# Expert weights with permuted rows, loaded in longer runs of HBM

## The chip, the cores and the metric

The kernel runs on one core of a Trainium2 chip, in one launch. The metric is the time of an execution on the device in microseconds (us). The core has five engines that run beside each other: TensorE (PE; its weight loads are listed apart as PEld), VectorE (DVE), ScalarE (ACT), GpSimd (POOL) and SyncE (SP), which here issues nearly all transfers. Sixteen DMA engines move the data between HBM and the core's on-chip memory (SBUF); matrix products land in PSUM. All data are float32.

## The reference, cut to what matters

Two blocks are applied to 256 tokens of 1024 channels, and each ends with a mixture of experts. The first has 16 experts with 256 inner channels, the second 32 experts with 512; each token goes to two experts of one group. Cut to the experts:

```python
for e in range(N_EXPERTS):
    act = jax.nn.silu(t @ w_gate[e]) * (t @ w_up[e]) * gates[:, e:e + 1]
    y = y + act @ w_down[e]
```

Here `t` holds the normalised tokens (in block 2 also scaled and shifted by columns that a modulation vector gives), `w_gate[e]` and `w_up[e]` are 1024 x 256 (block 2: 1024 x 512) and `w_down[e]` is 256 x 1024 (512 x 1024). Gate and up sum over the 1024 channels, down over the inner channels; a sum doesn't depend on the order of its terms.

## The kernel before, in words

The program works in stages: token mixing of block 1 (0 to about 150 us of the profile), its experts (to about 316 us), token mixing of block 2 (to about 840 us), and its experts (to the end). All experts' weights are streamed from HBM once, whatever the routing says.

**The lists.** For each expert the tokens' places in a list of 64 are worked out (`moe`, line 917, up to line 1009), which leaves PE partly idle at the start of both stages. `dispatch` (line 1062) gathers the listed tokens of four experts by a product with one-hot matrices: `xh` and `xl` are the normalised rows split in two parts (lines 926, 1000 and 1003, by ACT, POOL and DVE), and the result `xt[:, k, :]` holds 128 channels on the partitions for each of eight values of k. On the way out it is scaled by the norm column `gcol[:, k]` and, in block 2, shifted by `bcol[:, k]`.

**The products.** Experts are taken in pairs. `gate_up` (line 1111) forms gate and up from eight products over k for each of the two experts, then `act` (line 1131, DVE). `turn` (line 1134) transposes `act`, `down` (line 1142) multiplies by the down weights for two halves n of 512 output channels, each a sum over NF = 2 or 4 values of f, and `combine` (line 1162) adds the parts to the four sums `y` in PSUM. The order on PE is: gate and up of a pair, then the down product of the pair before it (`lower`, line 1194).

**The stream.** `Stream` (line 497) keeps the list of weight pieces of 1 MiB in the order of their use and issues their loads from SP, eight pieces ahead of the one that is wanted (`take`, line 541). A piece lies in a slot of 8 KB per partition of pool `gp`, which has 19 slots (NG) for all large tiles; a load waits until its slot is free. `load1` and `load2` (lines 550 and 557) say which rows of a weight matrix go to which partition: row 128 k + p to partition p, place k. So a partition reads single rows that lie 128 rows apart: 1 KB each for block 1's gate and up, 2 KB for block 2's gate and up, and 4 KB for block 1's down. Block 2's down weights are cut in two pieces by output columns, which makes 2 KB again; the first column half of `down` needs only the first piece of each expert. Slots are given out in the order of the loads, and SP issues in order. The last two pieces are loaded by halves in turn (line 527).

**The modulation.** `ada_job` (line 594) forms 512 of the modulation's values by products, turns them into columns by four transposes on PE (line 609) and adds the four parts and a bias on DVE (lines 610 and 611). Twelve of these jobs exist; numbers 6 to 8 run at the start of block 1's experts, where PE waits for the routing, number 9 in block 2's token mixing.

Of the kernel before, what the change touches and what calls it, by code (L numbers as in the profile page):

```python
# [122 lines left out]
def _body(es, tc, I, cst_d, msk_d, out_d, tap, stop):  # L123
# [73 lines left out]
    nA += 2  # L197
    colG = cp.tile([128, 8], F32, name="colG")
# [16 lines left out]
    def wload(ap, shape, name="w"):  # L215
        t = U(name, shape)
        SY.dma_start(t, ap)
        return t

    def piece(w, r0, nk, c0, n):  # L220
        """A piece of weights, split exactly into two parts that the PE array multiplies in one pass each."""
        hi = U("hi", [nk, n], F32R)
        lo = U("lo", [nk, n], F32R)
        for a in range(2):
            ks = slice(nk // 2 * a, nk // 2 * (a + 1))
            t = sp.tile([128, nk // 2, n], F32, tag="st4", name="w", bufs=NST)
            SY.dma_start(t, w[r0 + 64 * nk * a:r0 + 64 * nk * (a + 1), c0:c0 + n].rearrange("(k p) n -> p k n", p=128))
            t2["hi"] = A.activation(hi[:, ks], t, AF.Copy)  # L228
            t2["lo"] = V.tensor_tensor(lo[:, ks], t, hi[:, ks].bitcast(F32), op=ALU.subtract)  # L229
        return hi, lo  # L230

    class Jobs:
        """Products in the order of their use; the weights of the next ones are loaded and split ahead."""
# [22 lines left out]
        def ch(self, w, c0, h, n, evac):  # L256
            """out[channel, token]: evac(c, psum) for two groups of 128 channels."""
# [17 lines left out]
        def row32(self, w, c0, h, evac):  # L275
            """The same for two tiles, in float32 as it stands."""
# [15 lines left out]
        def row(self, w, c0, h, tiles, evac, n=512, keep=None, reuse=None, more=None):  # L292
            """out[token, channel]: evac(j, psum) for the tiles of 128 tokens."""
# [49 lines left out]
    def weave(main, sides, rate):  # L343
        """Traces main, with rate steps of the side chains between two of its steps."""
        due = 0.0
        sides = list(sides)
        for _ in main:
            due += rate
            while due >= 1.0 and sides:
                due -= 1.0  # L350
                g = sides.pop(0)
                try:
                    next(g)
                    sides.append(g)
                except StopIteration:
                    pass
        return sides
# [21 lines left out]
    def rms_h(x, behind=None):  # L379
        """The same, by halves of the rows."""  # L380
# [15 lines left out]
    def rms_r(x):  # L396
        """1 / root mean square of each row."""
# [30 lines left out]
    def transpose_split(x, r, hi, lo, off, gcol, bcol=None, ps=None, dg=None):  # L428
        """Rows scaled by r, transposed by a product with the diagonal of r."""
# [12 lines left out]
    class Router:  # L442
        """Logits of the experts, from the halves of the rows as they come."""
# [53 lines left out]
    class Stream:  # L497
        """Weight pieces of expert pairs, loaded in the order of their use and ahead of it."""
# [24 lines left out]
        def ahead(self, n):  # L523
            while self.n < min(n, len(self.order)):
                p, k, s, i = self.order[self.n]
                ap, shape = self.ap[p][k][s][i]
                if self.ends and self.n == len(self.order) - 2:
                    # the last two by halves in turn
                    two = [(U("w", shape), self.ap[p][k][q][i][0]) for q in range(2)]
                    for h in range(2):  # L530
                        for q, (t, ap) in enumerate(two):
                            SY.dma_start(t[:, 2 * h:2 * h + 2], ap[:, 2 * h:2 * h + 2])
                            self.t[(p, k, q, i)] = t
# [16 lines left out]
    def load1(e, kind):  # L550
        w = wsel(I[{"g": "w_gate", "u": "w_up", "d": "w_down"}[kind]], e)
        if kind == "d":
            return [(w.rearrange("(k p) n -> p k n", p=128), [2, D])]
        return [(w.rearrange("(k p) n -> p k n", p=128), [KD, 256])]

    st1 = Stream(load1, [(2 * p, 2 * p + 1) for p in range(8)])
    def load2(e, kind):
        w = wsel(I[{"g": "w_gate_2", "u": "w_up_2", "d": "w_down_2"}[kind]], e)
        wv = w.rearrange("(k p) n -> p k n", p=128)
        if kind == "d":  # L560
            return [(wv[:, :, 512 * i:512 * i + 512], [4, 512]) for i in range(2)]
        return [(wv[:, 4 * i:4 * i + 4, :], [4, 512]) for i in range(2)]

    st2 = Stream(load2, [(2 * p, 2 * p + 1) for p in range(16)], True)
    # ================= modulation and parameter columns of block 2 =================
# [13 lines left out]
    ada = cp.tile([128, 48, 2], F32, name="ada")  # L579

# [10 lines left out]
    def ada_job(jobs, b, step=False):  # L591
# [4 lines left out]
        def run(t0, t1):  # L596
# [11 lines left out]
            for c in range(4):  # L608
# [3 lines left out]
                            colC[:, oBA + 4 * b:oBA + 4 * b + 4].unsqueeze(2).to_broadcast([128, 4, 2]), op=ALU.add)  # L612
            yield
# [3 lines left out]
    # ================= block 1: token mixing =================  # L617
# [39 lines left out]
    # context tokens, normalised  # L657
# [77 lines left out]
    def conv_chain():  # L735
        # causal convolution
# [3 lines left out]
        # the last taps in another sum, by the idle engines  # L740
# [45 lines left out]
    def pool_chain():  # L786
        # windowed means
# [128 lines left out]
    # ================= mixture of experts =================  # L916
    def moe(x, E, router, gcol, bcol, st, FE, n_static, mid=None, before_if=None, gate=None, idle=None):
# [7 lines left out]
        xl = R2("xnl", F32R)  # L925
        for i in (1, 0):
            A.activation(xh[i], x[i], AF.Copy, scale=r[:, i:i + 1])
# [12 lines left out]
        # the group: first of the largest logits, and its probability  # L940
# [47 lines left out]
        # the place of each token in its expert's list  # L988
# [8 lines left out]
        for n in range(2):  # L997
# [3 lines left out]
            G.tensor_tensor(xl[1][:, cs], t, xh[1][:, cs].bitcast(F32), op=ALU.subtract)  # L1001
        with after(last_m):
            V.scalar_tensor_tensor(xl[0], x[0], r[:, 0:1], xh[0].bitcast(F32), op0=ALU.mult, op1=ALU.subtract)
# [10 lines left out]
        def spill():  # L1014
            # lists longer than CAP: further chunks
# [25 lines left out]
            # s2_ = 1 - offset of the chunk  # L1041
# [69 lines left out]
        def gate_up(gu, xt, off, wcol, half=None):  # L1111
# [19 lines left out]
            V.scalar_tensor_tensor(act, sg, wcol, outs[1], op0=ALU.mult, op1=ALU.mult)  # L1131
# [10 lines left out]
        def down(dn, aT):  # L1142
            parts = []
            for n in range(2):
                q = mm_ps("pdn")
                for f in range(NF):
                    for s in range(2):
                        pc = dn[s]
                        mm(q[64 * s:64 * s + 64, :], aT[:, f, 64 * s:64 * s + 64],
                           pc[n][:, f, :] if NF == 4 else pc[0][:, f, 512 * n:512 * n + 512], f == 0, f == NF - 1)  # L1150
# [104 lines left out]
    # ================= block 2: token mixing, its products in order =================  # L1255
# [12 lines left out]
    def mv_jobs():  # L1268
        # values of the mLSTM; first the context's, then the others
# [68 lines left out]
    def yb_job(kk):  # L1338
        # gate of the mLSTM's heads, and its output by channels
# [97 lines left out]
    y = moe(x1, 16, rt, colA[:, oFG:oFG + 8], None, st1, 256, 2, None, lambda: J2.ahead(1), idle=first_ada)  # L1437
# [8 lines left out]
    # ================= block 2: token mixing =================  # L1446
# [15 lines left out]
    # lower bounds of the forget gates  # L1462
# [40 lines left out]
    def gate_chain():  # L1503
        gA = U("gA", [4, 512])
        gB = U("gB", [4, 512])
        # rows 0-3: forward, rows 4-7: backward with time reversed; lat by columns of the grid
# [13 lines left out]
        # log sigmoid: min(x, 0) - log(1 + exp(-|x|)), the logarithm by its series in e / (2 + e)  # L1520
# [16 lines left out]
        # sums within tiles of 128  # L1537
# [54 lines left out]
    # short convolution of queries (lat by columns) and keys (lat by rows)  # L1592
# [109 lines left out]
    def gla_core(g):  # L1702
# [26 lines left out]
        for lv in range(8):  # L1729
            x = 1 << lv  # L1730
            m = 16 // x
            if x < 32:
                # within blocks of 32; both directions in one product: their keys and their queries lie in opposite halves
# [23 lines left out]
            # decay of the keys to the end of their half, of the queries from the start of theirs  # L1757
# [143 lines left out]
    V.tensor_copy(sh2, ada[:, 24:32, 0])  # L1901

# [22 lines left out]
    # ================= block 2: experts =================  # L1925
# [8 lines left out]
    y = moe(x3, 32, rt, mod2, sh2, st2, 512, 0, gate=gf[0], idle=last_ada)  # L1934
# [42 lines left out]
```

## Time and profile before

| | us |
|---|---|
| median of three runs | 1365.89 |
| lowest and highest | 1364.04, 1366.63 |
| span of the profiled execution (first to last instruction) | 1365.3 |
| PE busy, share of the span | 1269.9, 93% |
| DVE busy, ACT busy | 639.2, 432.4 |
| moved by DMA | 359.79 MB, mean 264 GB/s |

The profiled execution has no time of its own beside its span of 1365.3 us; it lies 0.6 us below the median of the runs. A matmul's end is modelled, so that "busy" on PE can cover short waits.

### The profile page before, as it was taken

The numbers are of one execution on the slowest core, as the hardware profiler recorded it, in microseconds if no ns is written. First come the engines' busy times: TensorE is split into PE (matmuls) and PEld (weight loads), VectorE is DVE, ScalarE is ACT, GpSimd is POOL, SyncE is SP. The second block draws the span as 40 slices with busy tenths as digits, with TensorE's granted clock in tenths as the row PEclk, the third lists the DMA queues.
The fourth block names the chain that finished last, engine by engine and source line by source line (L and its number), as shares of the span: only waits on it lengthen the run. The fifth ranks groups of instructions, "written<-read, shape, count | busy, mean of one in ns | idle before, by whom it ended". The sixth has DMA issues, their size and how long they took to land. (4 is left out here: it accounts for less than half of the span.)

```text
span 1365.3 us, 19881 instructions
## 1 busy us (share of the span) xinstructions
PE 1269.9 (93%) x8082; PEld 835.2 (61%) x8082; DVE 639.2 (47%) x1405; ACT 432.4 (32%) x756; POOL 37.6 (3%) x50
## 2 busy tenths in 40 slices
PE   6988899998999999999999999999998989797984
PEld 5845476666788988988988997444342424242421
DVE  6896531226388878776657665412111111111112
ACT  5735222224144745534345442111110101010101
POOL 4200100000000000000000001000000000000000
PEclk9989899999999999999999999999999999999998
DMA  8798899994332332424436679899999999999992
GB/s 266 249 337 294 276 303 360 366 341 146 108 93 62 93 93 67 142 80 124 128 93 205 235 245 353 307 389 390 390 389 387 390 390 390 390 387 390 393 390 108
DMA packets 226708, 359.79 MB, mean 264 GB/s; under 512 B 14200, under 2 KB 100385, under 8 KB 226608
## 3 DMA queue, kind: packets, MB, share of 16 engines
q1 hardware_dynamic: 217648, 355.49, 74.3%
q10 hardware_dynamic: 7952, 2.22, 0.7%
q8 instruction: 68, 1.11, 0.3%
q0 software_dynamic: 1008, 0.70, 0.2%
q14 instruction: 32, 0.26, 0.1%
HBM read 357.34 MB, written 1.05 MB: 263 GB/s over the span
## 5 line engine op out<-in xcount | busy, mean ns | idle before, releaser
L156 PE MATMUL pg<-hT,hi 128*128 128x256 f32 (+1 forms) x1024 | 233.0, 321 | 1.5 <-DVE Qg L1321 1.5
L156 PE MATMUL pgu<-w,XT 128*64 128x256 f32 (+1 forms) x1088 | 193.2, 483 | 14.5 <-DMA w<-in_w_up_dram 14.4
L156 PE MATMUL pdn<-w,actT 128*64 128x512 f32 x656 | 167.9, 597 | 10.4 <-DMA w<-in_w_down_dram 9.9
L156 PEld LDWEIGHTS pg<-hT,hi 128*128 128x128 f32 x1024 | 167.4, 188 | 16.3 <-DVE Qg L1321 1.7
L229 DVE TENSOR_TENSOR lo<-w,hi 128x1024 fp32r<-128x1024 f32 x122 | 145.8, 1219 | 47.3 <-ACT hi L228 19.4
L156 PE MATMUL pg<-hT,lo 128*128 128x256 f32 (+1 forms) x512 | 162.6, 318 | 0.0
L228 ACT ACTIVATE hi<-w 128x1024 fp32r<-128x1024 f32 x122 | 124.9, 1052 | 89.6 <-PE pr L156 32.1
L156 PEld LDWEIGHTS pgu<-w,XT 128*64 128x64 f32 x1088 | 80.8, 137 | 110.8 <-issue 68.3
L156 PE MATMUL pgg<-w,XT 128*64 128x512 f32 x512 | 134.6, 598 | 0.0
L156 PEld LDWEIGHTS pdn<-w,actT 128*64 128x64 f32 x656 | 51.0, 137 | 100.3 <-issue 78.1
L156 PEld LDWEIGHTS pg<-hT,lo 128*128 128x128 f32 x512 | 96.4, 189 | 7.4 <-issue 0.4
L1157 ACT ACTIVATE Ph<-Pg 128x512 fp32r<-128x512 f32 x32 | 20.1, 628 | 245.3 <-DVE Pg L1153 245.3
L156 PE MATMUL pr<-hi,hT 128*128 128x256 f32 (+1 forms) x384 | 91.0, 327 | 3.6 <-PEq L1231 3.6
L156 PEld LDWEIGHTS pgg<-w,XT 128*64 128x64 f32 x512 | 38.9, 137 | 71.0 <-issue 67.4
L1130 DVE TENSOR_TENSOR sgm<-sgm,pgg 128x512 f32<-128x512 f32 x16 | 11.0, 688 | 148.5 <-ACT sgm L1129 148.5
L1153 DVE TENSOR_TENSOR Pg<-pdn,g 128x512 f32<-128x512 f32 x32 | 22.1, 692 | 116.5 <-PE pdn L156 116.5
L156 PEld LDWEIGHTS pr<-hi,hT 128*128 128x128 f32 x384 | 65.5, 192 | 10.7 <-issue 4.0
L1131 DVE SCALAR_TENSOR_TENSOR act<-sgm,ws,pgu 128x512 f32<-128x512 f32 (+1 forms) x25 | 16.3, 652 | 106.7 <-PE pgu L156 106.3
L156 PE MATMUL pr<-lo,hT 128*128 128x256 f32 (+1 forms) x192 | 62.8, 327 | 0.0
L156 PE MATMUL py<-Ph,Gt 128*128 128x512 f32 x100 | 41.0, 441 | 18.4 <-ACT Ph L1157 16.9
L1139 ACT ACTIVATE actT<-pactT 128x512 f32<-128x512 f32 (+1 forms) x25 | 13.0, 519 | 132.4 <-PE pactT L1137 132.4
L156 PE MATMUL pgx<-Dd,xnh 128*128 128x256 f32 (+1 forms) x208 | 53.4, 297 | 0.3 <-DVE e L980 0.2
(515 smaller groups left out, 1934.3 us busy)
## 6 DMA issues: line engine op xcount, KB each, us to landing
w<-in_w_gate_dram SPq DMA_DIRECT2D x82, 1024.0 KB, 14.2
w<-in_w_up_dram SPq DMA_DIRECT2D x82, 1024.0 KB, 14.2
w<-in_w_down_dram SPq DMA_DIRECT2D x80, 1024.0 KB, 14.1
w<-in_w_in_dram SPq DMA_DIRECT2D x98, 512.0 KB, 4.5
w<-in_w_ada_dram SPq DMA_DIRECT2D x24, 1024.0 KB, 7.0
w<-in_w_out_dram SPq DMA_DIRECT2D x4, 1024.0 KB, 5.2
w<-in_w_branch_b_dram SPq DMA_DIRECT2D x8, 512.0 KB, 4.1
w<-in_w_branch_a_dram SPq DMA_DIRECT2D x8, 512.0 KB, 4.4
```

Source lines behind the costliest of these rows:

```text
L156: t2["mm"] = PE.matmul(out, lhsT, rhs, start=start, stop=stop, skip_group_check=True)
L228: t2["hi"] = A.activation(hi[:, ks], t, AF.Copy)
L229: t2["lo"] = V.tensor_tensor(lo[:, ks], t, hi[:, ks].bitcast(F32), op=ALU.subtract)
L1130: V.tensor_tensor(sg, sg, outs[0], op=ALU.mult)
L1131: V.scalar_tensor_tensor(act, sg, wcol, outs[1], op0=ALU.mult, op1=ALU.mult)
L1139: A.activation(aT, p, AF.Copy)
L1153: V.tensor_tensor(qg, q, gate[:, n, :], op=ALU.mult)
L1157: A.activation(ph, q, AF.Copy)
```

## The change

Weights are loaded so that partition p holds rows that lie next to each other: rows 4p to 4p+3 of each half of 512 rows for gate and up, rows 4p to 4p+3 of block 2's down weights (two pieces by rows instead of by columns), rows 2p and 2p+1 of block 1's. The run that a partition reads in one piece becomes 4 KB (block 1's gate and up) or 8 KB (the others). Everything that meets these rows follows the order: `xh` and `xl` are written with their columns permuted; `act` is written permuted; the norm columns are wanted in the new order, for which three small loads of runs of 16 bytes (`by_four`) and four more transposes, a sum and an addition in each of the jobs 6 to 9 are added; `down` reads its pieces by f instead of by n, so that both column halves need all pieces. Comments and docstrings were taken out too.

```diff
+    def by_four(name, ap):
+        n = ap.shape[0] // 512
+        t = cp.tile([128, 4 * n], F32, name=name)
+        A.dma_start(t.rearrange("p (h k) -> p h k", k=4), ap.rearrange("(h p k) -> p h k", p=128, k=4))
+        return t
...
-        SY.dma_start(t, ap)
+        SY.dma_start(t.rearrange("p (h k) n -> p h k n", h=2) if len(ap.shape) == 4 else t, ap)
...
-                            SY.dma_start(t[:, 2 * h:2 * h + 2], ap[:, 2 * h:2 * h + 2])
+                            SY.dma_start(t[:, h], ap[:, h])
...
-            return [(w.rearrange("(k p) n -> p k n", p=128), [2, D])]
-        return [(w.rearrange("(k p) n -> p k n", p=128), [KD, 256])]
+            return [(w.rearrange("(p k) n -> p k n", p=128), [2, D])]
+        return [(w.rearrange("(h p k) n -> p h k n", h=2, p=128), [KD, 256])]
...
-        wv = w.rearrange("(k p) n -> p k n", p=128)
         if kind == "d":
-            return [(wv[:, :, 512 * i:512 * i + 512], [4, 512]) for i in range(2)]
-        return [(wv[:, 4 * i:4 * i + 4, :], [4, 512]) for i in range(2)]
+            wv = w.rearrange("(p k) n -> p k n", p=128)
+            return [(wv[:, 2 * i:2 * i + 2, :], [2, D]) for i in range(2)]
+        return [(w[512 * i:512 * i + 512].rearrange("(p k) n -> p k n", p=128), [4, 512]) for i in range(2)]
...
+            if 6 <= b < 10:
+                q = mm_ps("paq", (4, 4, 32))
+                p4 = pt.rearrange("p (c k) -> p k c", k=4)
+                for c in range(4):
+                    PE.transpose(q[:, c].rearrange("p j a -> p (j a)"), p4[:, c, :], ident)
+                aq = adaq[:, 4 * b - 24:4 * b - 20]
+                V.tensor_reduce(aq, q[:, :, :, 0], op=ALU.add, axis=AX.X)
+                V.tensor_tensor(aq, aq, baq[:, 4 * b - 24:4 * b - 20], op=ALU.add)
...
+    fgq = by_four("fgq", I["ffn_norm_g"][0])
+    baq = by_four("baq", I["b_ada_2"][0, 3072:5120])
+    n2q = by_four("n2q", I["norm2_g_2"][0])
...
+        def q4(v, n=2):
+            return v.rearrange("p (h k c) -> p h c k", h=n, k=4)
+        def c4(v, n=2):
+            return v.rearrange("p (h c k) -> p h c k", h=n, k=4)
...
-            A.activation(xh[i], x[i], AF.Copy, scale=r[:, i:i + 1])
+            A.activation(q4(xh[i]), c4(x[i]), AF.Copy, scale=r[:, i:i + 1])
...
-            G.tensor_tensor(xl[1][:, cs], t, xh[1][:, cs].bitcast(F32), op=ALU.subtract)
+            G.tensor_tensor(q4(xl[1][:, cs], 1), c4(t, 1), q4(xh[1][:, cs].bitcast(F32), 1), op=ALU.subtract)
...
-            V.scalar_tensor_tensor(xl[0], x[0], r[:, 0:1], xh[0].bitcast(F32), op0=ALU.mult, op1=ALU.subtract)
+            for n in range(2):
+                cs = slice(512 * n, 512 * n + 512)
+                V.scalar_tensor_tensor(q4(xl[0][:, cs], 1), c4(x[0][:, cs], 1), r[:, 0:1],
+                                       q4(xh[0][:, cs].bitcast(F32), 1), op0=ALU.mult, op1=ALU.subtract)
...
-            V.scalar_tensor_tensor(act, sg, wcol, outs[1], op0=ALU.mult, op1=ALU.mult)
+            V.scalar_tensor_tensor(act.rearrange("p (f c) -> p c f", f=NF), sg.rearrange("p (c f) -> p c f", f=NF), wcol,
+                                   outs[1].rearrange("p (c f) -> p c f", f=NF), op0=ALU.mult, op1=ALU.mult)
...
-                           pc[n][:, f, :] if NF == 4 else pc[0][:, f, 512 * n:512 * n + 512], f == 0, f == NF - 1)
+                           pc[f // 2][:, f % 2, 512 * n:512 * n + 512], f == 0, f == NF - 1)
...
+    mod2q = cp.tile([128, KD], F32, name="mod2q")
+    V.scalar_tensor_tensor(mod2q, adaq[:, 8:16], 1.0, n2q, op0=ALU.add, op1=ALU.mult)
+    sh2q = adaq[:, 0:8]
```

The calls of `moe` get `fgq` in place of `colA[:, oFG:oFG + 8]`, and `mod2q, sh2q` in place of `mod2, sh2`; the router keeps the old columns.

## Rows read from the trace of the kernel before

**Rows 1.** Windows: busy us by engine, granted clock, DMA share, GB/s

```profile
core 0: us, PE busy (x) PEld busy (x) DVE busy (x) ACT busy (x) POOL busy (x), PEclk, DMA share, GB/s
245.00:280.00 35.00, 35.00 (x258) 23.60 (x255) 6.72 (x14) 7.28 (x16) 0.00 (x0) 1.00 1.07 369
...
860.00:864.00 4.00, 4.00 (x23) 1.58 (x23) 3.59 (x11) 2.04 (x3) 0.00 (x0) 1.00 0.00 0
...
872.00:1334.00 462.00, 422.07 (x1946) 166.93 (x1942) 73.60 (x124) 61.75 (x115) 0.00 (x0) 1.00 1.05 389
...
1338.00:1340.00 2.00, 2.00 (x10) 0.62 (x10) 0.00 (x0) 0.00 (x0) 0.00 (x0) 1.00 0.33 115
```

**Rows 2.** Waits from 866 to 1340 us: waited us, times, longest

```profile
PEld pgu L156 <- DMA w<-in_w_up_dram: 23.2, 10, 2.5
...
PEld pdn L156 <- DMA w<-in_w_down_dram: 17.9, 9, 2.5
```

**Rows 3.** Line 217 on SP's queue from 863 us: ns min/median/max, first and last

```profile
L217 SPq DMA_DIRECT2D w<-in_w_down_dram x61: 368/2530/4580, 864.1 to 1320.5; - x61
L217 SPq DMA_DIRECT2D w<-in_w_gate_dram x56: 367/2530/4580, 868.0 to 1293.8; - x56
L217 SPq DMA_DIRECT2D w<-in_w_up_dram x56: 368/2532/4577, 876.3 to 1304.1; - x56
```

**Rows 4.** Timeline of PE, two pairs of block 2: start, length, what

```profile
904.12 7.09 PE L156 MATMUL pgg<-w,XT 128*64 128x512 f32 x32
...
911.73 7.09 PE L156 MATMUL pgu<-w,XT 128*64 128x512 f32 x32
918.65 7.04 PE L156 MATMUL pdn<-w,actT 128*64 128x512 f32 x32
...
956.67 1.07 PE L156 MATMUL pgg<-w,XT 128*64 128x512 f32 x2
```

**Rows 5.** Waits from 150 to 320 us, of PE's down products

```profile
PEld pdn L156 <- ACT actT L1139: 1.2, 2, 0.8
...
PE pdn L156 <- ACT actT L1139: 0.5, 1, 0.5
```

**Rows 6.** Windows in which runs of one length fill the transfers

```profile
228.00:236.00 8.00, 8.00 (x69) 6.42 (x68) 0.91 (x3) 2.86 (x7) 0.00 (x0) 1.00 1.10 348
240.00:244.00 4.00, 4.00 (x24) 1.51 (x22) 1.59 (x3) 0.98 (x2) 0.00 (x0) 1.00 1.02 402
276.00:282.00 6.00, 6.00 (x46) 4.42 (x44) 0.20 (x1) 0.38 (x1) 0.00 (x0) 1.00 1.03 410
893.00:930.00 37.00, 37.00 (x191) 16.48 (x187) 7.98 (x13) 7.25 (x14) 0.00 (x0) 1.00 1.05 387
```

**Rows 7.** DMA queues (packets, MB, share) and one issue of ScalarE's

```profile
q10 hardware_dynamic: 7952, 2.22, 0.7%
...
mskf<-shape_masks ACTq DMA_DIRECT2D x1, 80.0 KB, 3.9
```

**Rows 8.** Timeline of PE at the start of block 1's experts

```profile
164.20 0.66 PE L609 MATMUL pac<-cst,adap 128*128 128x128 f32 x4 [2.92 <-ACT adap L606]
...
166.18 2.32 PE L156 MATMUL ppos<-Mr,cst 128*128 128x16 f32 x10
```

**Rows 9.** Groups by form: times, busy us, mean ns, idle before

```profile
L1287 ACT ACTIVATE mpre<-pg,colB 128x256 f32<-128x256 f32 x8 | 3.7, 468 | 24.0 <-PE pg L156 24.0
L1300 ACT ACTIVATE qsig<-pg,colB 128x256 f32<-128x256 f32 x8 | 3.7, 467 | 6.5 <-PE pg L156 6.5
L1003 DVE SCALAR_TENSOR_TENSOR xnl<-x,rry,xnh 128x1024 fp32r<-128x1024 f32 x2 | 2.6, 1276 | 0.0
L1001 POOL TENSOR_TENSOR xnl<-xn,xnh 128x512 fp32r<-128x512 f32 x4 | 5.0, 1258 | 0.0
```

**Rows 10.** Timeline of PE behind the last transfer, the last down product

```profile
1336.19 1.07 PE L156 MATMUL pdn<-w,actT 128*64 128x512 f32 x2
...
1337.85 5.36 PE L156 MATMUL pdn<-w,actT 128*64 128x512 f32 x22
```

More of the change, by code (lines that the diff above doesn't have):

```diff
@@ L579, in _body @@
     ada = cp.tile([128, 48, 2], F32, name="ada")
+    adaq = cp.tile([128, 16], F32, name="adaq")
     def param_cols():
@@ L1435, in first_ada @@
         drain(g)
-    y = moe(x1, 16, rt, colA[:, oFG:oFG + 8], None, st1, 256, 2, None, lambda: J2.ahead(1), idle=first_ada)
+    y = moe(x1, 16, rt, fgq, None, st1, 256, 2, None, lambda: J2.ahead(1), idle=first_ada)
     x2 = x1
@@ L1932, in last_ada @@
         yield
-    y = moe(x3, 32, rt, mod2, sh2, st2, 512, 0, gate=gf[0], idle=last_ada)
+    y = moe(x3, 32, rt, mod2q, sh2q, st2, 512, 0, gate=gf[0], idle=last_ada)
     ss = S("sf", [2, 2], bufs=1)
```

## Prediction

> **What bounds the kernel now.** First the windows, for what is full in which stage. In block 2's experts the DMA engines are busy all through: from 872 to 1334 us they move 389 GB/s without a break, while PE has 40 of 462 us idle [rows 1]. Second, the waits of that stretch, for who is late: PE's weight loads wait for up and down weights [rows 2], so transfers set the pace. The two other views agree. SP is never short of free slots there: one issue takes 2.5 us in the median [rows 3] because the transfers ahead of it are not yet taken up. And PE alone would be faster: while the pieces that were loaded ahead last, PE goes from the gate product of one pair at 904.12 to that of the second pair behind it at 956.67 [rows 4], 52.55 us for two pairs. Two pairs are 24 pieces of 1.0486 MB, 25.17 MB, which take 64.7 us at 389 GB/s. The stream begins after a pause of 4 us (no bytes from 860 to 864, since all slots were full [rows 1]) and its last bytes come in the window that ends at 1340 [rows 1]. In it lie 61 + 56 + 56 pieces [rows 3] and the last two, which another line loads by halves: 175 pieces, 183.5 MB. At 389 GB/s that is 471.7 us, about a third of the span of 1365.3 us.
>
> In block 1's experts it is otherwise. The DMA engines are as busy there (1.07, 369 GB/s), but PE is busy in 35.00 of 35 us [rows 1], and no row of that stage's waits has PE behind a transfer; its down products wait at most for ACT [rows 5]. So faster loads win nothing there, and what would be late next is PE itself. Token mixing of either block loads other weights, which the change leaves alone.
>
> **Does a run become one packet?** The queues say so. ScalarE's queue carried 7952 packets in 25 transfers [rows 7]. Counting by the code one packet for each run of HBM that is contiguous in all its dimensions gives 7552, and 16 more for each transfer give 7952 to the packet. The mask's load [rows 7] is written with three inner dimensions of 2, 5 and 16 numbers; cut by the innermost, it alone would be 1280 packets in place of 128, and the sum would be over the count. So adjacent dimensions merge, and the new pieces will be runs of 4 and 8 KB.
>
> **What a longer run is worth.** The windows of [rows 6] hold one length each: 1 KB in block 1's gate and up, 348 GB/s; 4 KB in block 1's down, 402 and 410 GB/s; 2 KB in block 2, 387 GB/s. With 16 engines that is for one packet 16 x 1024 / 348 = 47.1 ns, 16 x 2048 / 387 = 84.7 ns, and 16 x 4096 / 402 or 410 = 163.0 or 159.8 ns. The step from 1 to 2 KB is 37.6 ns per KB, with 9.5 ns left over for each packet. Carried on, it gives 159.9 ns at 4 KB, the better of the two rows, and 310.3 ns at 8 KB, which is 422 GB/s. The worse row makes the step from 2 to 4 KB 39.15 ns per KB, and 8 KB then 319.6 ns, or 410 GB/s. No row has 8 KB, so these are the bounds, 410 and 422; I take 416, between them. The stream is then 183.5 MB / 416 = 441.1 us, a gain of **30.6 us** (24.1 at 410, 36.9 at 422).
>
> [...]
>
> Does PE keep up? 25.17 MB at 416 GB/s are 60.5 us for two pairs, and PE needs 52.55; it would become the bound only at 479 GB/s. So PE's waits get shorter and transfers stay last.
>
> **The down product.** With the pieces cut by rows, both column halves need all four pieces of a pair, where the first half needed two. A matmul of it costs 7.04 / 32 = 0.22 us [rows 4]. At the end of the kernel PE is already behind the last bytes: 24 or more of the last 32 matmuls begin after 1336 us [rows 10], as the last bytes land. In the new order all but the first 8 or so would wait for the last pieces; that is the same 24, so I price it at 0, with 8 x 0.22 = 1.7 us as the upper bound. In the middle of the stream the later start is paid out of PE's slack; slots come free up to two pieces later, which SP's waiting issues cover.
>
> **What is added.** (a) Four jobs get four more transposes on PE. A group of four takes 0.66 us [rows 8], in stages where PE is on the path (jobs 6 and 7 stand ahead of the places' product that the routing ends with [rows 8]): 4 x 0.66 = 2.6 us. The two small DVE steps lie beside them. Below it would be 1.3, if the waits for ACT [rows 8] cover half. (b) Three loads of runs of 16 bytes, 256 + 512 + 256 = 1024 packets at the start, on ScalarE's queue. That queue's 7952 packets took 0.7% of the engines' span [rows 7], 9.6 us or 1.2 ns each, so 1.2 us at most, and they stand in front of the first weights; I take 1.0. (c) The permuted writes. An ACT step that reads in a permuted order takes 468 ns, its plain neighbour 467 [rows 9]; so 0 for ACT. For DVE `xnl` becomes two steps where one took 1276 ns [rows 9], 0.1 us more. For POOL no row shows a stride; from 0 to twice its 1258 ns for two steps [rows 9], 2.5 us a stage. I take 0, because POOL works beside the routing's chain on DVE; without that cover it is 2.5 us in each stage. The permuted `act` lies, in block 2, under PE's wait for weights. Nothing new stands in SP's queue. Sum: +3.7 us, from 2 to 9.
>
> **The sum.** -30.6 + 3.7 = -26.9 us: the span goes from 1365.3 to 1338.4, and with the 0.6 us by which the median of the runs lies above it, the forecast is **1339 us**, with 1331 to 1351 as its own bounds (-36.9 + 2 and -24.1 + 9).
>
> **The rivals.** (1) Four KB is the end: a packet of 8 KB gains nothing over two of 4 KB. Then the rate is 402 to 410, in the middle 406, and the stream 452.0 us: 1365.9 - 19.7 + 3.7 = 1350 (1354 at 402). For it: the lower of the two 4 KB rows already lies under the straight line. Against: the step from 2 to 4 KB is still there in both. Chance 0.22.
> (2) The down product's wait becomes PE's bound. Each pair waits for two more pieces, 2 x 2.52 us at 416 GB/s, and PE finds nothing to do in their place: 26.3 + 5.0 = 31.3 us a pair against 30.3 for the transfers. Over 175 / 12 = 14.6 pairs that is 457 us, a gain of 15 us: 1355. Against: the sums over the first two pieces can run meanwhile, and a wait that PE makes up later costs nothing. Chance 0.08.
> (3) Slower: the run's length doesn't matter above 2 KB, and only the added work is left: 1365.9 + 3.7 = 1369.6. It decides from a rate at 8 KB of 392 GB/s downward, where the 471.7 us shrink by less than 3.7. For it: no row has 8 KB, and sixteen engines that each read one long run meet HBM in another order. Against: the three lengths of [rows 6], each faster than the one before. Chance 0.07. [...]
> (4) That the change doesn't do what it says (runs stay at 2 KB): the same 1369.6, but the packet count is against it; 0.01, in (3)'s.
>
> **How the numbers follow.** The forecast's case has 0.60, the rivals 0.22, 0.08 and 0.07, something better than its bound 0.03. The range of 8 in 10 takes in the forecast's bounds and both rivals that end on the same side, and leaves out (3): 1329 to 1357. A measurement here can tell about 0.2%, 2.7 us. Faster: 0.60 + 0.22 + 0.08 + 0.03, less 0.03 for a gain that is eaten up: 0.90; same 0.03; slower 0.07.
>
> **What would show it.** The packets of SP's queue fall to about half. Windows in block 2's experts read 410 to 422 GB/s; at 402 to 410 it is rival 1, at 389 rival 3. The stream's last bytes come near 1312. In rival 2 the DMA share falls below the level of before within the stream while PE's rows show longer waits for down weights. The start of block 1's experts is 1 to 3 us later. Block 1's experts keep their length; if they get shorter, transfers did bound them and the reading of [rows 5] was wrong.

## The result

The changed kernel takes 1342.88 us (median of four runs, 1341.91 to 1343.69), 0.9828 of the kernel before (95% interval 0.9815 to 0.9841). The forecast was 1339 with a range of 1329 to 1357. Its profiled execution has a span of 1340.1 us, 25.2 less than before; that span lies 2.8 us below the median (the execution itself took 1341.91 us, 1.8 more than its span).

The transfers first: windows of the changed kernel, the same columns as in [rows 1].

```profile
872.00:1300.00 428.00, 421.22 (x1914) 170.27 (x1912) 76.50 (x123) 62.87 (x114) 0.00 (x0) 1.00 1.01 422
...
1304.00:1306.00 2.00, 2.00 (x12) 0.78 (x10) 0.00 (x0) 0.00 (x0) 0.00 (x0) 1.00 0.46 186
1306.00:1308.00 2.00, 2.00 (x12) 0.91 (x10) 0.00 (x0) 0.00 (x0) 0.00 (x0) 1.00 0.01 4
```

The rate is 422 GB/s where it was 389, the upper end of the forecast's bounds. PE is busy in 421 of 428 us; before it had 40 of 462 us idle. The last bytes come at about 1304.9 us (0.9 us of the window to 1306 at 422 GB/s), before at about 1338.6. The queues' packets, to be read beside [rows 7]:

```profile
q1 hardware_dynamic: 114224, 355.49, 69.8%
q10 hardware_dynamic: 9024, 2.24, 0.8%
```

SP's queue had 217648 packets before, 103424 more. Counted by the code, one packet for each run gives the same difference (block 1 loads the weights of 18 experts and block 2 those of 32, and the halves of the last two pieces are runs of 4 KB, not 8), so the new runs are one packet each. ScalarE's queue has 1072 more: 1024 runs of 16 bytes and 16 for each of three transfers, as counted. SP's loads in block 2's experts answer to [rows 3]:

```profile
L224 SPq DMA_DIRECT2D w<-in_w_down_dram x61: 327/328/384, 866.6 to 1281.8; - x61
L224 SPq DMA_DIRECT2D w<-in_w_gate_dram x56: 327/328/384, 870.4 to 1257.0; - x56
L224 SPq DMA_DIRECT2D w<-in_w_up_dram x56: 327/328/474, 878.7 to 1269.4; - x56
```

An issue takes 328 ns where it took 2530, which was near the 2.70 us of a piece at 389 GB/s. That it took so long because the transfers ahead were not yet taken up was my reading; no row names it. What SP still waits for is a free slot: from 866 to 1300 us the profile ends 224 us of its waits with a product of PE and 134 us with a load. And PE's waits for weights, 23.2 and 17.9 us in [rows 2], are nearly gone:

```profile
PEld pgu L156 <- DMA w<-in_w_gate_dram: 2.9, 10, 0.3
PEld pgg L156 <- DMA w<-in_w_down_dram: 1.1, 5, 0.3
PEld pdn L156 <- DMA w<-in_w_up_dram: 1.0, 5, 0.3
```

So the bound has moved: PE is now as late as the transfers. Windows from one whole cycle of two pairs, first the pair with dispatch, then the one without, then both:

```profile
1109.78:1144.53 34.75, 33.51 (x154) 14.70 (x153) 6.05 (x11) 6.46 (x12) 0.00 (x0) 1.00 1.01 421
1144.53:1169.10 24.57, 24.57 (x109) 8.78 (x109) 4.48 (x6) 2.45 (x4) 0.00 (x0) 1.00 1.01 422
1109.78:1169.10 59.32, 58.08 (x261) 23.48 (x261) 10.53 (x17) 8.91 (x16) 0.00 (x0) 1.00 1.01 422
```

PE's cycle takes 59.3 us (58.1 busy, the rest waits for DVE), the transfers 25.17 MB / 422 GB/s = 59.6 us. Pieces had been loaded ahead when PE began, PE never works that lead off, and so much is left to do when the last bytes are there. The last two down products, to be read beside [rows 10]:

```profile
1303.44 7.08 PE L156 MATMUL pdn<-w,actT 128*64 128x512 f32 x28
1312.96 1.07 PE L156 MATMUL pdn<-w,actT 128*64 128x512 f32 x2
1314.62 7.09 PE L156 MATMUL pdn<-w,actT 128*64 128x512 f32 x30
```

The last one ends 17 us behind the last bytes, before it ended 9 us behind them. The sum of the two traces: the stream (first issue to last bytes) 438.3 us instead of 474.5, -36.2; its start 866.6 instead of 864.1, +2.5; what is left behind the last bytes 35.2 us instead of 26.7, +8.5. Together -25.2.

The permuted writes answer to [rows 9] (L954 was L927, L1028 was L1001, L1032 was L1003):

```profile
L1161 DVE SCALAR_TENSOR_TENSOR act<-sgm,ws,pgu 128x512 f32<-128x512 f32 x16 | 17.8, 1110 | 86.8 <-PE pgu L156 86.8
L954 ACT ACTIVATE xnh<-x,rry 128x1024 fp32r<-128x1024 f32 x4 | 8.0, 2090 | 2.3 <-DVE rry L383 2.3
...
L1028 POOL TENSOR_TENSOR xnl<-xn,xnh 128x512 fp32r<-128x512 f32 x4 | 6.0, 1527 | 0.0
L1032 DVE SCALAR_TENSOR_TENSOR xnl<-x,rry,xnh 128x512 fp32r<-128x512 f32 x4 | 4.4, 1104 | 0.0
```

Plainly written, they took 748, 1142, 1258 and, for both halves at once, 1276 ns.

### The profile page after: what moved, and what is told of

It is laid out like the page before. It is cut to its first block, busy times and chain, and to the rows that moved or that the text cites. A ratio compares the mean times of both kernels' runs of the same rounds, so it can differ in the third digit from the quotient of the medians.

```text
span 1340.1 us, 19921 instructions
## 1 busy us (share of the span) xinstructions
PE 1278.2 (95%) x8098; PEld 842.5 (63%) x8098; DVE 647.4 (48%) x1416; ACT 437.5 (33%) x756; POOL 38.7 (3%) x50
## 3 DMA queue, kind: packets, MB, share of 16 engines
HBM read 357.35 MB, written 1.05 MB: 267 GB/s over the span
## 5 line engine op out<-in xcount | busy, mean ns | idle before, releaser
L156 PE MATMUL pgu<-w,XT 128*64 128x256 f32 (+1 forms) x1088 | 190.3, 481 | 0.0
L156 PE MATMUL pdn<-w,actT 128*64 128x512 f32 x656 | 180.6, 596 | 0.5 <-ACT actT L1170 0.5
L156 PE MATMUL pgg<-w,XT 128*64 128x512 f32 x512 | 127.1, 596 | 0.0
L156 PEld LDWEIGHTS pdn<-w,actT 128*64 128x64 f32 x656 | 56.0, 137 | 93.9 <-issue 85.7
L1161 DVE SCALAR_TENSOR_TENSOR act<-sgm,ws,pgu 128x512 f32<-128x512 f32 (+1 forms) x25 | 23.8, 952 | 87.2 <-PE pgu L156 86.8
L1119 ACT ACTIVATE XT<-pgx,adaq,mod2q 128x256 f32<-128x256 f32 x60 | 30.0, 562 | 96.3 <-PE pgx L156 96.3
L156 PEld LDWEIGHTS pgx<-Dd,xnh 128*128 128x128 f32 x208 | 40.3, 195 | 20.4 <-issue 13.7
```

The costliest lines, as they stand in the source:

```text
L156: t2["mm"] = PE.matmul(out, lhsT, rhs, start=start, stop=stop, skip_group_check=True)
L1119: A.activation(xt[:, k, 0:w], p[:, j, :], AF.Identity, scale=gcol[:, k:k + 1], bias=bcol[:, k:k + 1])
L1161: V.scalar_tensor_tensor(act.rearrange("p (f c) -> p c f", f=NF), sg.rearrange("p (c f) -> p c f", f=NF), wcol, outs[1].rearrange("p (c f) ...
```

## The experiments

Two questions were open. What made PE's cycle 59.3 us: the later `act` on DVE, or the new order of the down product? And did the run's length, or PE, set the end? The kernel before took 1367 to 1370 us beside these kernels, so ratios to it are compared. The changed kernel itself ran among them:

> The changed kernel itself, on the chip of the three kernels that follow, so that they can be set against it directly. Every theory: 0.983 of the kernel before.

1341.99 us, 0.9807 (0.979 to 0.9824).

**The loads alone.** The kernel before, with this in place of its loads, and `down` reading by f:

```diff
+            wv = w.rearrange("(p k) n -> p k n", p=128)
+            return [(wv[:, 2 * i:2 * i + 2, :], [2, D]) for i in range(2)]
+        return [(w[512 * i:512 * i + 512].rearrange("(p k) n -> p k n", p=128), [4, 512]) for i in range(2)]
```

> The kernel before with block 2's experts' weights alone loaded in runs of 8 KB (down weights cut by rows); nothing follows the permuted rows: xh, xl, act, norm columns and block 1 stay as before, so block 2's experts multiply rows with channels that don't belong to them. Theory (the gain is the transfers' rate alone, and half of what the rate gives is lost again on PE, because with pieces cut by rows the down product's matmuls no longer alternate between the two experts): 421 to 422 GB/s from 872 to 1300 us, first gate product at 860.5 us, 2.4 us earlier than in the changed kernel, two pairs still take about 59 us on PE, and the median is about 1340 (1338 to 1342), 2 to 3 us below the changed kernel. Rival (the permuted write of act, 0.36 us longer on DVE in front of the next one-hot matrices, makes PE slow): without that write two pairs take 55 us, the last work behind the last bytes shrinks from 34.6 to about 27 us, and the median is 1333.

1338.61 us, 0.9794 (0.9777 to 0.981). One cycle of two pairs:

```profile
1080.91:1139.99 59.08, 58.11 (x262) 23.49 (x261) 9.90 (x17) 8.91 (x16) 0.00 (x0) 1.00 1.01 422
```

Without any permuted write the cycle is shorter by only 0.2 us, so `act` on DVE isn't what slows PE. By the ratios (0.9807 and 0.9828 for the changed kernel), all that the change adds beside these loads costs 2 to 5 us; the interval of the first ratio overlaps with that of this kernel, so the size stays open.

**The down product with alternating experts.** In the changed kernel both column halves read the same pieces, and its list of PE's instructions puts expert 0's piece to use in both halves before expert 1's: the experts follow each other as 0 0 1 0 1 1 0 1. In a pair with dispatch, the dispatch's matmuls are set in between, and the product falls into four parts:

```profile
1123.14 1.45 PE L156 MATMUL pdn<-w,actT 128*64 128x512 f32 x3
...
1127.00 3.65 PE L156 MATMUL pdn<-w,actT 128*64 128x512 f32 x12
1132.08 1.93 PE L156 MATMUL pdn<-w,actT 128*64 128x512 f32 x4
1135.52 3.65 PE L156 MATMUL pdn<-w,actT 128*64 128x512 f32 x12
```

(The profile counts two for each matmul of the program, 32 for the 16 of a pair's down product.) The four at 1132.08 are two of the program's, both of expert 0, and each of the four takes 0.47 us (the dispatch goes on at 1133.94), where [rows 4] has 0.22. Fixed order:

```diff
+            qs = [mm_ps("pdn") for _ in range(2)]
+            prev = None
+            for f0 in range(0, NF, 2):
+                for n in range(2):
+                    for f in (f0, f0 + 1):
+                        for s in range(2):
+                            with after(prev) if prev is not None and NF == 4 else nullcontext():
+                                prev = mm(qs[n][64 * s:64 * s + 64, :], aT[:, f, 64 * s:64 * s + 64],
+                                          dn[s][f // 2][:, f % 2, 512 * n:512 * n + 512], f == 0, f == NF - 1)
...
```

> The changed kernel with the order of block 2's down product on PE fixed so that neighbouring matmuls belong to different experts (first two rows f of both column halves, then the last two); all else as changed. Theory (in the changed kernel the sequence of experts is 0 0 1 0 1 1 0 1, matmuls of the same expert stand next to each other and can't run side by side on the array's two column halves; that costs 0.8 us in a pair without dispatch and 3 to 4 us in one with it): two pairs go from 59.3 to 54 to 55 us, transfers stay at 422 GB/s and end near 1305 us, PE waits for weights again, the work behind the last bytes shrinks from 34.6 to about 27 us, and the median is 1335 to 1337, 6 to 8 us below the changed kernel's 1342.9. Rival (the order costs nothing; PE's pace comes from the later act and one-hot matrices on DVE): 59 us and 1342 to 1344. Second rival (PE's pace doesn't matter, transfers alone set the end): two pairs get shorter and the median stays at 1342 to 1344.

1330.13 us, 0.973 (0.9711 to 0.9749): 10 to 13 us faster than the changed kernel, with the same loads and the same work. A cycle, and the end:

```profile
1102.64:1159.94 57.30, 57.13 (x261) 22.97 (x260) 10.36 (x17) 8.69 (x16) 0.00 (x0) 1.00 1.01 421
```

```profile
1301.77 1.07 PE L156 MATMUL pdn<-w,actT 128*64 128x512 f32 x2
1303.43 7.08 PE L156 MATMUL pdn<-w,actT 128*64 128x512 f32 x30
```

The cycle is 2.0 us shorter. The product of a pair without dispatch takes 7.45 us in both kernels; in the pair with dispatch its rows add up to 11.1 us in the changed kernel and to 9.2 here. Six of the sixteen down products are cut by a dispatch, which makes 12 us. The last down product starts 11.2 us earlier, where PE has caught up with the transfers (it waits 1.32 us for down weights at 1290.60), whose end hardly moved (1304.3 us). That the order costs time holds, its size for one cycle doesn't: I had expected 54 to 55 us and a loss in every pair.

**All of one expert, then all of the other.** The same order as a list, `seq`, sorted by expert:

```diff
+            seq = [(s, f0 + f, n) for f0 in range(0, NF, 2) for n in range(2) for f in range(2) for s in range(2)]
+            for s, f, n in (sorted(seq, key=lambda q: q[0]) if NF == 4 else seq):
...
```

> The changed kernel with the order of block 2's down product fixed the other way: all sixteen matmuls of one expert, then all sixteen of the other, so that next to no neighbours belong to different experts. Work, loads and pieces are those of the kernel with alternating experts (1330 us). Theory (matmuls of different experts fill different column halves of the PE array and run side by side, 0.22 us each in the profile's count; neighbours of the same expert run one after the other, 0.43 to 0.465 us each): the 32 of a pair take 14 to 15 us instead of 7.1, two pairs 72 to 73 us instead of 57.3, PE alone sets the end, 16 x 7 to 7.8 us are added, and the median is 1435 to 1455. Rival (neighbours of one expert cost nothing, and what the fixed order gained came from the column halves being finished in another order or from fewer breaks by the dispatch): 1328 to 1335.

1388.41 us, 1.0142 (1.0125 to 1.0158), 56 to 58 us more than with alternating experts (by the ratios and by the medians) and half of what was expected. The down product of a pair without dispatch, which nothing interrupts:

```profile
1183.99 11.81 PE L156 MATMUL pdn<-w,actT 128*64 128x512 f32 x31
```

31 in 11.81 us are 0.38 us each, against 0.24 (31 in 7.45 us) when the experts alternate. So neighbours of the same expert do cost: each is 0.59 us long in the profile's count, whichever the order, and those of different experts, which write different 64 of the 128 output rows, overlap more. That two of them run side by side on two halves of the array was my picture of it, which no row shows. And 0.38, not 0.47, is the price in an unbroken row; the changed kernel's 0 0 1 0 1 1 0 1 costs nothing in the pair without dispatch (7.45 us as well). It loses only in the pair where dispatch cuts the row and leaves matmuls of one expert alone (11.1 us against 9.2).

**Runs of 4 KB.**

```diff
-            wv = w.rearrange("(p k) n -> p k n", p=128)
+            wv = w.rearrange("(k p) n -> p k n", p=128)
...
-        return [(w[512 * i:512 * i + 512].rearrange("(p k) n -> p k n", p=128), [4, 512]) for i in range(2)]
+        return [(w[512 * i:512 * i + 512].rearrange("(h p k) n -> p h k n", h=2, p=128), [4, 512]) for i in range(2)]
```

> The changed kernel with block 2's weights loaded in runs of 4 KB instead of 8 KB (two rows each for gate and up, single rows of 4 KB for down); the products still follow the order of the 8 KB runs, so rows of block 2's weights meet channels of other rows. Theory (each packet costs 9.5 ns beside 37.6 ns per KB): 402 to 410 GB/s from 872 to 1300 us, so transfers are last again: last bytes 9 to 18 us later than 1305, PE waits for weights, work behind the last bytes near 27 us, median 1345 to 1353. Rival (4 KB is the end of the gain): 420 GB/s and above, 1342 to 1344. Second rival (PE's pace of 59.3 us for two pairs hides the difference): 410 GB/s or a little less, and 1343 to 1345.

1341.97 us, 0.9812 (0.9795 to 0.983), the same as with 8 KB. Windows of the stream, of the last bytes and of a cycle:

```profile
872.00:1300.00 428.00, 421.25 (x1915) 170.29 (x1913) 76.34 (x122) 62.87 (x114) 0.00 (x0) 1.00 1.03 410
...
1316.00:1318.00 2.00, 2.00 (x12) 0.72 (x10) 0.00 (x0) 0.00 (x0) 0.00 (x0) 1.00 0.33 133
```

```profile
1109.59:1168.89 59.30, 58.06 (x261) 23.51 (x261) 10.53 (x17) 8.91 (x16) 0.00 (x0) 1.00 1.03 411
```

The second rival is right: the rate is 410, the last bytes come 12 us later, and the time doesn't move, because PE keeps its 59.3 us and only the rest behind the last bytes shrinks, from 35.2 to 24.6 us. In the changed kernel the step from 4 to 8 KB is worth nothing. It also settles rival 1 of the prediction: 4 KB is not the end of the rate.

**Slots at multiples of 256 bytes.** In the kernel before the slots of 8224 bytes start at 24128, so one of the sixteen that carry the stream starts at a multiple of 256. Its loads unchanged, with

```diff
+    V.memset(cp.tile([128, 48], F32, name="pad"), 0.0)
...
-    mv = t2["mv"] = [U("mv", [2, 4, 257]) for _ in range(2)]
+    mv = t2["mv"] = [U("mv", [2, 4, 264]) for _ in range(2)]
...
```

> The kernel before, its loads and its order untouched, with the slots of the large tiles moved: the pool starts at a multiple of 256 bytes in SBUF and each slot has 8448 bytes instead of 8224 (the value tile gets rows of 264 numbers instead of 257). In the kernel before one of the sixteen slots that the weights go through starts at a multiple of 256 bytes, and the profile shows a burst of 408 GB/s about every sixteen pieces. Theory (a packet of 2 KB that starts off such a boundary costs some 4 ns more): 405 to 410 GB/s for 2 KB runs all the time, stream 20 to 23 us shorter, transfers still last, median 1342 to 1347. Rival (the bursts have another cause): 387 to 390 GB/s and 1364 to 1367.

1344.28 us, 0.983 (0.9813 to 0.9846): as much as the whole change, from where the slots lie. The stream, and a cycle:

```profile
872.00:1300.00 428.00, 405.69 (x1902) 161.18 (x1898) 71.43 (x121) 60.90 (x114) 0.00 (x0) 1.00 1.05 408
```

```profile
1102.68:1160.99 58.31, 55.80 (x262) 22.18 (x261) 9.98 (x17) 8.55 (x17) 0.00 (x0) 1.00 1.05 408
```

Runs of 2 KB move at 408 GB/s instead of 389, 80.3 instead of 84.2 ns a packet. This cycle also shows PE's own pace with the order of the kernel before, while the transfers (25.17 MB / 408 GB/s = 61.7 us) are still ahead of it: 58.31 us, of which 55.80 busy and 2.51 in two waits of `py` for ACT's `Ph`.

The edit also makes the slots longer, so the start alone is not yet shown to be the cause. The kernel before settles it, with its slots untouched: its rate rises for some 4 us in every 43 (931 to 935, 974 to 979, 1017 to 1022 us), which is the time of sixteen pieces at 389 GB/s, and one slot of sixteen starts at a multiple of 256.

```profile
937.00:973.00 36.00, 36.00 (x174) 15.36 (x172) 6.48 (x12) 6.69 (x13) 0.00 (x0) 1.00 1.05 387
976.00:977.00 1.00, 1.00 (x8) 0.32 (x6) 0.21 (x1) 0.00 (x0) 0.00 (x0) 1.00 1.06 412
```

The change itself moves the pool to 24352, which leaves one slot of sixteen at such a multiple again; so its 422 GB/s are owed to the runs and not to the slots.

**Where the permutation is paid.** First `act` written plainly, and read with a stride by its transposes:

```diff
...
-                PE.transpose(p[:, f, :], act[:, 128 * f:128 * f + 128], ident)
+                PE.transpose(p[:, f, :], act.rearrange("p (c f) -> p f c", f=NF)[:, f, :], ident)
...
```

> The changed kernel with the down product's order fixed (neighbouring matmuls of different experts) and act written plainly again; the four transposes of turn read it with a stride of 16 bytes instead. Theory (the permuted write costs DVE 0.36 us a pair, but nothing waits for it longer than it is covered): act back to 0.75 us on DVE, two pairs 57 us as with the fixed order alone, median the same as with the fixed order alone, 0.973 of the kernel before within 0.1%. Rival (the next one-hot matrices stand behind act on DVE and PE waits for them): 0.4 us less per pair with dispatch, 3 us in all, 0.971. Second rival (PE reads a strided act more slowly): transposes go from 0.28 us to up to 0.56 us each, 64 of them, and up to 9 us are lost.

1331.19 us, 0.9735 (0.9716 to 0.9754), no difference. `act` is back at 748 ns; the weight loads that now read it take 203 instead of 140 ns, which the time doesn't show. Then `xh` and `xl` as well, read with a stride by dispatch's weight loads:

```diff
...
-                        mm(p[:, j, :], s[i][:, 128 * k:128 * k + 128], d[:, i]
+                        mm(p[:, j, :], s[i].rearrange("p (h c k) -> p h k c", h=2, k=4)[:, k // 4, k % 4, :], d[:, i]
...
```

> The same, and xh and xl written plainly too; dispatch's weight loads read their 128 channels with a stride of 16 bytes instead. Theory (the permuted writes of xh and xl by ACT and DVE are what makes the first gate product of block 2's experts later, 862.9 us against 860.5 us before): xnh back to 1.14 us and xnl on DVE to 1.28 us, first gate product 2 to 3 us earlier, and of block 1 1 to 2 us, median 2 to 4 us below the kernel with plain act alone. Rival (weight loads with a stride are slower, 0.19 us to 0.38 us for each of the 32 of a dispatch): 8 dispatches of block 2 and 4 of block 1 lose up to 6 us each where PE is the bound, and it is slower. Second rival (the later start is covered, since transfers set the end): the same.

1372.64 us, 1.0036 (1.0024 to 1.0049), 41 us lost and slower than the kernel before. The rows of dispatch's weight loads, which take 188 and 189 ns in the changed kernel:

```profile
L156 PEld LDWEIGHTS pgx<-Dd,xnl 128*128 128x128 f32 x128 | 42.3, 330 | 10.0 <-issue 10.0
L156 PEld LDWEIGHTS pgx<-Dd,xnh 128*128 128x128 f32 x128 | 42.1, 329 | 6.5 <-PE pdn L156 4.1 <-issue 2.4
```

The rival is right. Dispatch's matmuls follow each other every 0.24 us instead of 0.12, on PE, which is the bound (busy in 60.69 of 60.69 us of a cycle): block 1's experts take 164 us from their first gate product to block 2's first product, where they take 145 in the other kernels. The same with aligned slots:

> The same, with the slots of the large tiles at multiples of 256 bytes (8448 bytes each). Theory (each packet that starts off such a boundary costs 4 to 5 ns more, whatever its length): 16 x 8192 bytes / (310.6 - 4.3 ns) = 428 GB/s instead of 422, the stream 6 us shorter; but PE needs 57 us for two pairs, 25.17 MB at 428 GB/s take 58.8 us, so transfers stay last by a little, and the median falls by 3 to 6 us. Rival (PE sets the end): 428 GB/s and the same time. Second rival (only short packets gain): 422 GB/s and the same time.

1373.51 us, 1.004 (1.0025 to 1.0055): 426 GB/s where the transfers run freely, and no gain, because PE is the bound (busy in 416.6 of the 418 us from 872 to 1290).

Last, the permutation on the reading side of the same DVE, ACT and POOL instructions:

```diff
-            return v.rearrange("p (h k c) -> p h c k", h=n, k=4)
+            return v.rearrange("p (h k c) -> p h k c", h=n, k=4)
...
-            return v.rearrange("p (h c k) -> p h c k", h=n, k=4)
+            return v.rearrange("p (h c k) -> p h k c", h=n, k=4)
...
```

> The changed kernel with the down product's order fixed, and with the permutations of xh, xl and act turned round: each of the same instructions walks in the order in which it writes, so that it writes neighbouring numbers and reads with a stride of 16 bytes. Theory (a write with a stride is what costs, a read with a stride is free, as the two ACT steps of 468 and 467 ns in the kernel before say): xnh 2.07 back to 1.14 us, xnl on DVE 1.1 to 0.65 us, on POOL 1.51 to 1.26 us, act 1.11 to 0.75 us; first gate product of block 2's experts 2 to 3 us earlier than with the fixed order alone (861.8 us); median 2 to 4 us below the fixed order alone, 0.970 to 0.9715 of the kernel before. Rival (a stride costs the same on either side): durations and time stay as with the fixed order alone, 0.973. Second rival (durations fall, but the later start was covered by the transfers): 0.973.

1329.70 us, 0.9716 (0.9689 to 0.9743), not told apart from the fixed order alone. Groups:

```profile
L1161 DVE SCALAR_TENSOR_TENSOR act<-sgm,ws,pgu 128x512 f32<-128x512 f32 x16 | 20.1, 1258 | 88.2 <-PE pgu L156 88.2
...
L954 ACT ACTIVATE xnh<-x,rry 128x1024 fp32r<-128x1024 f32 x4 | 8.5, 2176 | 2.3 <-DVE rry L383 2.3
...
L1161 DVE SCALAR_TENSOR_TENSOR act<-sgm,ws,pgu 128x256 f32<-128x256 f32 x9 | 4.4, 484 | 0.4
```

The writes of the changed kernel step by 512 bytes from one number to the next, these reads by 16. The reads cost as much as the writes or a little more (2176 against 2090 ns, 1258 against 1110); the theory falls. Block 1's `act` steps by 8 bytes as a read, which costs nothing (484 against 481 ns plain); its write, which steps by 512 bytes too, cost 671.

**The fastest.** The fixed order with aligned slots, and with the reads too:

> The changed kernel with the down product's order fixed and the slots of the large tiles at multiples of 256 bytes (8448 bytes each). Theory (a packet of 8 KB that starts off such a boundary costs about 4 ns more): 426 to 427 GB/s instead of 422, the stream 5 us shorter; two pairs take 57.3 us on PE and 58.9 us on the transfers, so transfers are still last: median 3 to 5 us below the fixed order alone, 0.9695 to 0.971 of the kernel before. Rival (PE is last by now): 426 GB/s and 0.973.

> All three: the down product's order fixed, permutations on the reading side, slots at multiples of 256 bytes. Theory (the two gains add up, since one lies before the stream and the other in it): 5 to 9 us below the fixed order alone, 0.9665 to 0.9695 of the kernel before, 1321 to 1326 us. Rival (the start of the stream is set by free slots and not by the first gate product, and PE is last): 0.972 to 0.973.

1327.32 us, 0.9698 (0.9677 to 0.9718), and 1324.49 us, 0.968 (0.9659 to 0.9701). The stream of the first:

```profile
872.00:1290.00 418.00, 416.98 (x1924) 167.54 (x1922) 75.63 (x123) 61.56 (x114) 0.00 (x0) 1.00 1.01 427
```

8 KB runs gain too, 307.0 instead of 310.6 ns a packet. Both are faster than either kernel. The first interval still overlaps with that of the fixed order alone (0.9711 to 0.9749), and the second with the first, so what the slots and what the reads each add to the fixed order's time stays open.

## Why the prediction was right

The time came out 3.9 us above the forecast and well inside the range, but the terms were off and cancelled, and that the sum came so close is luck: the stream 5.6 us shorter than forecast, what is left behind the last bytes 8.5 longer, the added work 1.2 shorter (2.5 for 3.7), and the median 2.8 us above the span for 0.6.

- **What bounds the kernel before, and block 1.** Right. Faster transfers alone (slots_aligned) gave 23 us, and block 1's experts kept their length: 144.6 us before and 145.3 after from first gate product to block 2's first product.
- **One run, one packet.** Right, to the packet.
- **The rate.** The line through 1 and 2 KB [rows 6] was right at both lengths, 410 at 4 KB and 422 at 8 KB; I took 416, and the stream gained 36.2 us instead of 30.6. Against rival 3, no length up to 8 KB was without gain. But part of the line's 9.5 ns a packet belongs not to the packet but to where it lands: slots at multiples of 256 bytes take some 4 ns off at 2 and at 8 KB (80.3 for 84.2, 307.0 for 310.6).
- **"PE needs 52.55 us; transfers stay last."** This step failed. The stretch of [rows 4] is no whole cycle: it runs from a gate product behind a combine to one ahead of the next, and holds 254 matmuls, where a cycle has 261 (the missing ones are seven of `py`). The cycle that begins where it ends, from 956.67 to 1014.67, takes 58.0 us in the kernel before, and no wait in it is for weights: 55.5 us are busy, and 2.5 us `py` waits for ACT's `Ph`.

```profile
956.67:1014.67 58.00, 55.49 (x261) 22.20 (x261) 9.99 (x18) 8.56 (x17) 0.00 (x0) 1.00 1.05 388
PE py L156 <- ACT Ph L1157: 2.5, 2, 1.4
```

  So PE was 2.5 us below the forecast's 60.5 and not 8. The cycle of the changed kernel, with another order of matmuls in the down product, is 1.3 us longer again: 59.3 beside the 59.6 us of the transfers.
- **The down product at 0 (upper bound 1.7 us).** The step that failed most: what is left behind the last bytes grew by 8.5 us. I had weighed a wait, and there was hardly one (`pdn` waits 1.0 us for weights in all); the cost came from the order on PE. It is rival 2's place and result (PE as the bound) by another mechanism. Against the order of the kernel before, its price is 1.3 us in each of six cycles, by estimate 8 us; against alternating experts it is the 10 to 13 us between the two kernels. Rival 2 itself, waits of 5 us a pair for down pieces, is not in the trace.
- **(a) and (b), 3.6 us.** Not seen: block 1's experts start at 174.38 us, before at 175.00. In the other profiles they start at 170.47 to 177.58 us with (a) and (b), and at 172.98 and 173.06 without, so it can't be told what the two cost.
- **(c) permuted writes at 0.1 us.** Wrong in size. The rows I chose [rows 9] show an ACT step that reads PSUM with a stride; these write SBUF with one. From the last router product to the first dispatch matmul of block 2 it was 11.64 us before and is 13.48 (11.64 to 12.39 in all kernels that write plainly, 13.47 to 13.68 in all that permute on ACT, DVE and POOL). Two steps of `xnl` of 1.1 us stand ahead of the places on DVE, where one of 1.28 stood. And POOL's `xnl`, taken at 0 because it lies beside the routing's chain, is not without effect there, as far as the rows tell: two steps of DVE that run beside it take 1.32 and 1.45 us, before 1.05 and 1.19, as POOL's two steps go from 2.48 to 3.00 us, while the first of the two on DVE, done again when POOL is idle, takes 0.23 (before 0.22). The 1.8 us is most of the later start of the stream (+2.5). The first step, before and after:

```profile
848.76 1.05 DVE L955 TENSOR_TENSOR f1o<-f1o,f1c 128x64 f32<-128x64 f32 x1
849.02 1.32 DVE L982 TENSOR_TENSOR f1o<-f1o,f1c 128x64 f32<-128x64 f32 x1
```

Of the strides in these rows, reads that step by 16 bytes cost (`xnh` 2176 ns instead of 1142, `act` 1258 instead of 748), reads that step by 8 don't (484 against 481), and the writes that step by 512 bytes cost as well (2090 instead of 1142, 671 instead of 481). Why, no run shows.

## What to carry to other kernels

Before a bound is called far away, measure the next engine's cycle from a point to the same point one cycle later, count its instructions, and let its waits for other engines stand in it: seven missing matmuls and 2.5 us of such waits were 5.4 of the 8 us of margin. When a piece of data is cut in another direction, ask not only who waits longer but which order the engine's instructions will take, and whether neighbours that overlapped still do. Compare a strided access with a row that has the same stride, on the same side, in the same memory.

## What was not expected of the hardware

- Where a run lands in SBUF brought as much time here as its length: 2 KB runs went from 389 to 408 GB/s, 8 KB runs from 422 to 427, when the slots were laid at multiples of 256 bytes. That is some 4 ns a packet, whether it has 2 or 8 KB (80.3 for 84.2, 307.0 for 310.6); its cause was not tried further.
- In the profile's count, down matmuls of two experts in turn take 0.24 us each, those of one expert in an unbroken row 0.38, and pairs of one expert cut off by other products 0.47.
- Two steps of DVE took 1.05 and 1.19 us beside POOL's `xnl`, where the first of them alone took 0.22, and 1.32 and 1.45 when POOL's two steps took 3.00 us for 2.48.
- Dispatch's weight loads took 330 instead of 189 ns with a stride of 16 bytes, and that cost 41 us.
